# Head-norm factors and their selectors held on 128 partitions instead of 48

## The chip, the cores and the metric

The kernel runs on one core of one Trainium2 chip. It is written in a tile framework that orders the instructions of each engine and places the semaphores. The metric is the device time of one execution in microseconds (us); the time of a kernel is the median of several runs. PE is TensorE (its weight loads are listed apart, as PEld), DVE is VectorE, ACT is ScalarE, SP issues most of the transfers.

## The reference

The program is a first block (attention with dilated windows, a state-space branch and a feed-forward part, all over 256 positions of width 1024) and then a second block of two layers over two streams, x and a context c, of 256 positions each. What matters here is in the mixers of the second block: each head of the queries and keys is normalized over its own 64 (or 64 and 32) features before it is rotated and used.

```
def rms_norm(x, gain=None):
    xf = x.astype(jnp.float32)
    y = xf * lax.rsqrt(jnp.mean(xf * xf, axis=-1, keepdims=True) + EPS)
    if gain is not None:
        y = y * gain.astype(jnp.float32)
    return y.astype(x.dtype)
...
    aq = apply_rope2d(rms_norm(aq.reshape(B, S, A_HEADS, HEAD_DIM), a_q_norm), *rope)
    ak = apply_rope2d(rms_norm(ak.reshape(B, S, A_KV_HEADS, HEAD_DIM), a_k_norm), *rope)
...
    bq = diff_qk(bq, b_q_norm, rope)
    bk = diff_qk(bk, b_k_norm, rope)
...
    dq = rms_norm(dq.reshape(B, S, D_HEADS, HEAD_DIM), d_q_norm)
    dk = rms_norm(dk.reshape(B, S, D_HEADS, HEAD_DIM), d_k_norm)
```

## The kernel before

Activations lie with the features on the partitions and the 256 positions in the free dimension, one tile of 128 features x 256 positions per block. A projection is a row of units. Each unit takes one 128 x 1024 slab of weights (loaded by SP, split into a high part on ACT, line 120, and a low part on DVE, line 121) and multiplies it on TensorE in three products per block of the contraction (lines 139, 140 and 141): 512 columns wide where both streams are taken together, 256 where one is, and 320 or 256 columns in the value projections (lines 1153 to 1155, and 1510 to 1512 for `c_v`).

The mixers `mix_ab` (layer 0) and `mix_cd` (layer 1) run the head norms, class `HeadNorm`, as steps that are queued behind the units (`K.later`) and so fall between the products of later units on TensorE:

- `square_sums`: small products over the squares of a block (line 1035, 2 columns) give the sum of squares of each of its two heads, for each position.
- `spread`: the reciprocal roots of all heads of a group, with positions on the partitions, are transposed (line 1044) to one row per head, `n` rows (10, 8 or 2). `K.split` writes a high part to rows 0 to `n` and a low part to rows 32 to 32+`n` of a tile of the ring `rh`. All other rows hold zeros, written once by `stacked`.
- `finish`: one product per output with a selector of ones and zeros spreads each head's factor over its partitions, in a PSUM tile `pt` (two buffers, which the transposes use too), and DVE multiplies the block by it, at once with its gain (line 1061), or after the rotation (lines 1065 to 1069).

```
            cs = slice(i * 128 + rr.start, i * 128 + rr.stop)
            nc.tensor.matmul(r, self.sel[:, cs], self.r, start=True, stop=True)
            if rope is None:
                nc.vector.scalar_tensor_tensor(o, o, gain[:m], r, op0=ALU.mult, op1=ALU.mult)
```

This product, line 1059, contracts over the partitions of the two tiles, 48. Its moving operand is `rh`, 256 columns, and its stationary operand the selector, `m` columns wide. There are 64 such products. In `mix_ab` there are 26, all with m = 128. In `mix_cd` there are 38: 8 for `dk` and 4 for `dq` with m = 128, 2 for `kr` and 8 for the queries `cq` with m = 96, and 16 for `kn` with m = 64, two per block since a block's two heads go to different places of `kc`.

The selectors are loaded by `head_selectors` from the ACT queue (line 1083) and cast on DVE (line 1084), once in `mix_ab` and twice in `mix_cd`; the ring of four tiles is cleared on ACT (line 1095) in each mixer. The order of the work on each engine comes from the framework and doesn't depend on these sizes.

Of the kernel before, what the change touches and what calls it, by code (L numbers as in the profile page):

```python
# [9 lines left out]
F32R = mybir.dt.float32r  # L10
# [6 lines left out]
T = 256  # L17
# [1058 lines left out]
def head_selectors(K, pool, width, rows, n):  # L1076

    nc, A = K.nc, K.A
    at, n2 = COLS[f"sum{width}"]
    sums = K.cols[:rows, at:at + n2]  # L1080
    raw = K.raw_p.tile([128, 1024], F32, name="wraw")
    sel = pool.tile([48, n * 128], F32R, name=f"sel{width}")
    nc.scalar.dma_start(raw[:48, :n * 128], A[f"sel{width}"])
    nc.vector.tensor_copy(sel, raw[:48, :n * 128])
    return sums, sel


def stacked(K, pool):

    zero = K.t1("zero")  # L1090
    K.nc.vector.memset(zero, 0.0)
    ring = []
    for i in range(4):
        ring.append(pool.tile([48, T], F32R, name=f"rh{i}"))
        K.nc.scalar.copy(ring[i], zero[:48])
    return ring


# [70 lines left out]
def mix_ab(K, streams):  # L1169
# [14 lines left out]
    rctx = ExitStack()  # L1184
    rp = K.pool(rctx, "abr", 1)
    s64, sel64 = head_selectors(K, rp, 64, 128, 5)
    ring = stacked(K, rp)
    cos, sin = K.t1("cos"), K.t1("sin")
    nc.scalar.dma_start(cos, A["rope_cos"])
# [209 lines left out]
def mix_cd(K, streams):  # L1399
# [28 lines left out]
    tctx = ExitStack()  # L1428
    tp = K.pool(tctx, "cdt", 1)
    s64, sel64 = head_selectors(K, tp, 64, 128, 5)  # L1430
    s96, sel96 = head_selectors(K, tp, 96, 96, 4)
    ring = stacked(K, tp)

    rank = {("q", "x"): 6, ("k", "x"): 2, ("k", "c"): 2}
# [304 lines left out]
def constants():  # L1739
    import numpy as np  # L1740
    f = np.float32
    c = {}
    i = np.arange(128)
    c["ident"] = np.eye(128, dtype=f)
    c["tri"] = (i[:, None] <= i[None, :]).astype(f)
    for g, d in ((1, 4), (2, 16)):
        seg = T // d
        ok = (i[:, None] // seg == i[None, :] // seg) & (i[:, None] >= i[None, :])
        c[f"mask{g}"] = np.where(ok, 0.0, NEG).astype(f)

    def bucket(dist):
        dist = np.asarray(dist)
        big = 16 + (np.log(np.maximum(dist, 1).astype(f) / f(16)) / f(math.log(2048 / 16)) * f(16)).astype(np.int32)
        return np.where(dist < 16, dist, np.minimum(big, 31))

    oh = np.zeros((33, 896), f)
    for g, (c0, n, off, d) in enumerate(((0, 383, 255, 1), (384, 255, 127, 4), (640, 255, 127, 16))):
        u = np.arange(n)
        oh[np.where((off - u >= 0) & (off - u <= 128), bucket(np.clip(off - u, 0, 128) * d), 32), c0 + u] = 1.0
    c["onehot"] = oh  # L1760
    sel = np.zeros((8, 512), f)
    for h in range(8):
        sel[h, h * 64:h * 64 + 64] = 1.0
    c["sel"] = sel
    for name, rows, n in (("sel64", [64, 64], 5), ("sel96", [64, 32], 4)):
        sel = np.zeros((48, n, 128), f)
        for b in range(n):
            at = 0
            for e, r in enumerate(rows[:2]):
                sel[[2 * b + e, 32 + 2 * b + e], b, at:at + r] = 1.0  # L1770
                at += r
        c[name] = sel.reshape(48, n * 128)
    t = np.arange(T)

    def rope(dim):
        nf = dim // 4
        inv = (f(10000.0) ** (-np.arange(nf, dtype=f) / f(nf))).astype(f)
        ang = np.concatenate([(t // 64).astype(f)[:, None] * inv, (t % 64).astype(f)[:, None] * inv], axis=-1)
        cos, sin = np.cos(ang.astype(np.float64)).astype(f), np.sin(ang.astype(np.float64)).astype(f)
        full = lambda a, sign: np.stack([sign * a.reshape(T, 2, nf), a.reshape(T, 2, nf)], axis=2).reshape(T, dim).T  # L1780
        return full(cos, 1), full(sin, -1)

    cos, sin = rope(64)
    c["rope_cos"], c["rope_sin"] = np.tile(cos, (2, 1)), np.tile(sin, (2, 1))
    cos, sin = rope(32)
    c["mla_cos"] = np.concatenate([np.ones((64, T), f), cos])
    c["mla_sin"] = np.concatenate([np.zeros((64, T), f), sin])
    q, k = i[:, None], i[None, :]
    c["amask"] = np.stack([np.where(k + 128 - q <= 128, 0.0, NEG), np.where(q + 128 - k <= 128, 0.0, NEG)], 1).astype(f)
    cq = np.tile(np.arange(64), 2)[:, None]  # L1790
    ck = np.tile(np.arange(64), 4)[None, :]
    start = np.clip(cq - 8, 0, 48)
    c["dmask"] = np.where((ck >= start) & (ck < start + 16), 0.0, NEG).astype(f)
    return {k: np.ascontiguousarray(v, dtype=f) for k, v in c.items()}


def prepare(inp):
    import numpy as np
    f = np.float32
    I = {k: np.asarray(v) for k, v in inp.items()}  # L1800
    out = constants()
    feat = lambda a: np.ascontiguousarray(a.reshape(T, KB, 128).transpose(2, 1, 0))
    out["x"], out["ctx"] = feat(I["x"][0]), feat(I["ctx_2"][0])
# [101 lines left out]
```

## Time and profile before

| | |
|---|---|
| median of 3 runs | 2502.96 us (2500.68 to 2505.42) |
| profiled execution | 2511.2 us, of which the span of the program's instructions is 2509.1 us |
| TensorE | busy 2440.5 us, 97% of the span |
| VectorE, ScalarE, GpSimd | busy 1641.9, 1067.5 and 20.6 us |
| mean granted TensorE clock | 0.986 of full speed |

The profiled execution is a single one, 8.2 us above the median; 2.1 us of its time lie outside its span. Busy time of TensorE is modelled: a matmul's record ends when its result is expected, and the next one's begins before that, so the spacing of starts tells more than the durations.

### The profile page before, as it was taken

How to read it: one execution, taken by the hardware profiler on the slowest of the kernel's cores; microseconds unless marked ns; L12 is line 12 of the kernel's file. 1: busy time of each engine (PE TensorE's matmuls, PEld its weight loads, DVE VectorE, ACT ScalarE, POOL GpSimd, SP SyncE). 2: the span in 40 equal slices, each digit the busy share in tenths (PEclk: the TensorE clock that was granted, in tenths of full speed). 3: DMA queues.
4: the chain of work that ended last, by engine and by line, in shares of the span. 5: the costliest groups of instructions: out<-in, count | busy, mean ns of one | idle time of the engine just before them, and what ended most of it. 6: DMA issues, size and time to landing. Idle time of an engine off the chain costs nothing.

```text
span 2509.1 us, 38385 instructions
## 1 busy us (share of the span) xinstructions
PE 2440.5 (97%) x15104; PEld 2097.5 (84%) x15104; DVE 1641.9 (65%) x3012; ACT 1067.5 (43%) x1934; POOL 20.6 (1%) x30
## 2 busy tenths in 40 slices
PE   6999999999999999999999999999999999999999
PEld 5999899999888888886598888887888888866999
DVE  4667787787855675768757666657545455767555
ACT  4667565545522222536743222243222234555443
POOL 1000000000000000000000000000000000000000
PEclk9999899999999999999899999999999999999999
DMA  8555455676444554331025555434555422332554
GB/s 248 161 154 168 137 168 186 203 250 223 160 155 143 162 177 127 122 125 51 1 68 158 161 160 160 155 97 148 171 166 161 142 87 81 108 91 80 177 185 127
DMA packets 117252, 363.83 MB, mean 145 GB/s; under 512 B 21170, under 2 KB 28658, under 8 KB 117072
## 3 DMA queue, kind: packets, MB, share of 16 engines
q1 hardware_dynamic: 114512, 355.73, 44.8%
q0 software_dynamic: 1280, 3.45, 0.7%
q8 instruction: 119, 1.95, 0.3%
q10 hardware_dynamic: 1280, 2.20, 0.3%
q14 instruction: 61, 0.50, 0.1%
HBM read 359.33 MB, written 3.82 MB: 145 GB/s over the span
## 4 chain that ended last, share of the span: by engine, by line
PE 69%; DVE 4%; ACT 2%; issue 1%; DMA 0%; ACTq 0%; DVEq 0%; SPq 0%
PE pm L139 20%; PE pm L140 20%; PE pm L141 20%; PE pt L1128 1%; PE pa L1035 1%; DVE wl L121 1%; PE pm L1327 1%; PE pt L1059 1%; PE pa L1579 1%; PE pm L1587 1%; DVE al L362 1%; PE pa L1343 1%; DVE y L357 1%; PE pm L1267 1%; PE pa L1304 0%
## 5 line engine op out<-in xcount | busy, mean ns | idle before, releaser
L139 PE MATMUL pm<-ah,wh 128*128 128x256 f32 (+2 forms) x3096 | 1007.7, 328 | 25.3 <-ACT ah L361 11.0
L140 PE MATMUL pm<-al,wh 128*128 128x256 f32 (+2 forms) x3096 | 1001.8, 324 | 1.5 <-DVE al L362 1.5
L141 PE MATMUL pm<-ah,wl 128*128 128x256 f32 (+2 forms) x3096 | 999.9, 324 | 0.0
L120 ACT CAST wh<-wraw 128x1024 fp32r<-128x1024 f32 (+4 forms) x535 | 540.4, 1013 | 1028.8 <-PE pm L140 833.4
L121 DVE TENSOR_TENSOR wl<-wraw,wh 128x1024 fp32r<-128x1024 f32 (+4 forms) x535 | 627.4, 1176 | 245.9 <-ACT wh L120 243.4
L139 PEld LDWEIGHTS pm<-ah,wh 128*128 128x128 f32 (+1 forms) x3096 | 587.2, 191 | 87.4 <-ACT ah L361 12.5
L140 PEld LDWEIGHTS pm<-al,wh 128*128 128x128 f32 (+1 forms) x3096 | 591.2, 191 | 56.1 <-DVE al L362 2.8
L141 PEld LDWEIGHTS pm<-ah,wl 128*128 128x128 f32 (+1 forms) x3096 | 588.8, 190 | 52.9 <-issue 1.7
L140 PE MATMUL pm<-hl,wh 128*128 128x512 f32 (+1 forms) x934 | 316.5, 339 | 0.4 <-DVE hl L126 0.4
L139 PE MATMUL pm<-hh,wh 128*128 128x512 f32 (+1 forms) x934 | 316.0, 338 | 0.7 <-DVE xx L449 0.7
L141 PE MATMUL pm<-hh,wl 128*128 128x512 f32 (+1 forms) x934 | 315.9, 338 | 0.0
L989 DVE SCALAR_TENSOR_TENSOR junk<-wraw,cactc 128x1024 f32<-128x1024 f32 x112 | 137.1, 1224 | 187.7 <-DMA wraw<-w_mod 187.5
L989 DVE SCALAR_TENSOR_TENSOR junk<-wraw,cactx 128x1024 f32<-128x1024 f32 x144 | 176.0, 1222 | 40.9 <-DMA wraw<-w_mod 38.3
L140 PEld LDWEIGHTS pm<-hl,wh 128*128 128x128 f32 x934 | 176.4, 189 | 22.2 <-DVE hl L126 0.6
L139 PEld LDWEIGHTS pm<-hh,wh 128*128 128x128 f32 x934 | 175.7, 188 | 22.4 <-issue 0.8
L141 PEld LDWEIGHTS pm<-hh,wl 128*128 128x128 f32 x934 | 175.6, 188 | 21.5
L125 ACT CAST hh<-g 128x512 fp32r<-128x512 f32 (+1 forms) x113 | 59.3, 526 | 183.8 <-DVE g L419 183.8
L419 DVE TENSOR_TENSOR g<-g,pm 128x512 f32<-128x512 f32 (+1 forms) x113 | 64.0, 566 | 69.8 <-PE pm L141 67.9
L126 DVE TENSOR_TENSOR hl<-g,hh 128x512 fp32r<-128x512 f32 (+1 forms) x113 | 63.8, 566 | 0.3
L449 DVE SCALAR_TENSOR_TENSOR xc<-pm,mcol0c,xc 128x256 f32<-128x256 f32 x56 | 26.9, 481 | 56.0 <-PE pm L141 55.9
L415 ACT ACTIVATE g<-pm 128x512 f32<-128x512 f32 (+1 forms) x116 | 56.0, 487 | 1.4 <-PE pm L141 1.4
L1128 PEld LDWEIGHTS pt<-ident,e 128*128 128x128 f32 x272 | 30.7, 145 | 22.1 <-issue 18.8
(423 smaller groups left out, 2243.4 us busy)
## 6 DMA issues: line engine op xcount, KB each, us to landing
wraw<-w_mod SPq DMA_DIRECT2D x144, 512.0 KB, 3.9
wraw<-f1g SPq DMA_DIRECT2D x44, 512.0 KB, 3.7
wraw<-f1u SPq DMA_DIRECT2D x44, 512.0 KB, 4.2
wraw<-f2g SPq DMA_DIRECT2D x44, 512.0 KB, 3.7
wraw<-f2u SPq DMA_DIRECT2D x44, 512.0 KB, 4.0
wraw<-f1d SPq DMA_DIRECT2D x32, 512.0 KB, 4.2
wraw<-f2d SPq DMA_DIRECT2D x32, 512.0 KB, 3.6
wraw<-w_xbc SPq DMA_DIRECT2D x24, 512.0 KB, 3.6
```

Source lines behind the costliest of these rows:

```text
L120: nc.scalar.copy(h[:, :f], raw[:, :f])
L121: nc.vector.tensor_tensor(lo[:, :f], raw[:, :f], h[:, :f].bitcast(F32), op=ALU.subtract)
L125: self.nc.scalar.copy(h, src)
L126: self.nc.vector.tensor_tensor(lo, src, h.bitcast(F32), op=ALU.subtract)
L139: nc.tensor.matmul(out, h[:, c], ah, start=first, stop=False)
L140: nc.tensor.matmul(out, h[:, c], al, start=False, stop=False)
L141: nc.tensor.matmul(out, lo[:, c], ah, start=False, stop=last)
L415: nc.scalar.activation(half(g["g"], s), p, AF.Silu)
L419: nc.vector.tensor_tensor(t, t, p, op=ALU.mult)
L449: self.nc.vector.scalar_tensor_tensor(x, p, gate, x, op0=ALU.mult, op1=ALU.add)
L989: nc.vector.scalar_tensor_tensor(junk, raw, 1.0, K.cact[s], op0=ALU.mult, op1=ALU.mult, accum_out=K.mcol[layer, s][:, j:j + 1])
L1128: nc.tensor.transpose(p[:, j * 128:(j + 1) * 128], b, K.ident)
```

## The change

The tiles of the ring `rh` and of the selectors get 128 partitions instead of 48. The arrays `sel64` and `sel96` in memory get 128 rows, the added ones zero, so the loads, the casts and the clearing are over 128 partitions too. The product of line 1059 then contracts over 128 partitions, of which 80 hold zeros on both sides. Its result is the same sum. No instruction is added, removed or moved on any engine: the lists of before and after differ only in the shapes of the casts, the clearing and the three loads, and in the operands of the 64 products.

```
-    sel = pool.tile([48, n * 128], F32R, name=f"sel{width}")
-    nc.scalar.dma_start(raw[:48, :n * 128], A[f"sel{width}"])
-    nc.vector.tensor_copy(sel, raw[:48, :n * 128])
+    sel = pool.tile([128, n * 128], F32R, name=f"sel{width}")
+    nc.scalar.dma_start(raw[:, :n * 128], A[f"sel{width}"])
+    nc.vector.tensor_copy(sel, raw[:, :n * 128])
...
-        ring.append(pool.tile([48, T], F32R, name=f"rh{i}"))
-        K.nc.scalar.copy(ring[i], zero[:48])
+        ring.append(pool.tile([128, T], F32R, name=f"rh{i}"))
+        K.nc.scalar.copy(ring[i], zero)
...
-        sel = np.zeros((48, n, 128), f)
+        sel = np.zeros((128, n, 128), f)
...
-        c[name] = sel.reshape(48, n * 128)
+        c[name] = sel.reshape(128, n * 128)
```

## Rows read from the trace of the kernel before

**Rows 1.** The page: busy time and share of each engine.
```profile
PE 2440.5 (97%) x15104; PEld 2097.5 (84%) x15104; DVE 1641.9 (65%) x3012; ACT 1067.5 (43%) x1934; POOL 20.6 (1%) x30
```

**Rows 2.** Windows: us, busy (count) PE, PEld, DVE, ACT, POOL, PE clock, DMA share, GB/s.
```profile
1088.00:1153.00 65.00, 64.87 (x356) 53.96 (x355) 44.42 (x137) 17.48 (x42) 0.00 (x0) 1.00 0.21 74
1153.00:1300.00 147.00, 140.23 (x807) 94.65 (x806) 101.60 (x286) 97.14 (x242) 0.00 (x0) 0.95 0.09 29
2130.00:2220.00 90.00, 90.00 (x623) 76.91 (x622) 60.95 (x161) 41.88 (x101) 0.00 (x0) 1.00 0.35 112
```

**Rows 3.** Line 1059: durations in ns (min/median/max), starts, forms.
```profile
L1059 PE MATMUL pt<-rh,sel x64: 275/357/386, 1090.7 to 2216.9; 48*128 48x256 f32 x38, 48*64 48x256 f32 x16, 48*96 48x256 f32 x10
```

**Rows 4.** Timeline of TensorE in mix_cd, a selector product among 256-column products: start, duration.
```profile
2151.60 0.28 PE L140 MATMUL pm<-lq,wh 128*96 128x256 f32 x1
2151.81 0.38 PE L1059 MATMUL pt<-rh,sel 48*128 48x256 f32 x1
2152.12 0.36 PE L141 MATMUL pm<-hq,wl 128*96 128x256 f32 x1
2152.32 0.28 PE L139 MATMUL pm<-hq,wh 128*96 128x256 f32 x1
```

**Rows 5.** Timeline of TensorE in mix_ab, a selector product among 320-column products.
```profile
1145.17 0.31 PE L1154 MATMUL pa<-wh,al 128*128 128x320 f32 x1
1145.41 0.38 PE L1059 MATMUL pt<-rh,sel 48*128 48x256 f32 x1
...
1145.97 0.30 PE L1153 MATMUL pa<-wh,ah 128*128 128x320 f32 x1
```

**Rows 6.** Timeline of TensorE in mix_ab, a pair of selector products before a 512-column unit.
```profile
1097.67 0.50 PE L1059 MATMUL pt<-rh,sel 48*128 48x256 f32 x2
...
1098.44 0.40 PE L140 MATMUL pm<-al,wh 128*128 128x512 f32 x1
```

**Rows 7.** Timeline of TensorE, a product over 96 rows behind one over 128.
```profile
2153.96 0.28 PE L141 MATMUL pm<-hq,wl 128*96 128x256 f32 x1
2154.08 0.50 PE L1035 MATMUL pa<-cols,sq 96*128 96x2 f32 x4
```

**Rows 8.** Timeline of TensorE, a 64-wide selector product (kn).
```profile
2162.59 0.28 PE L139 MATMUL pm<-hq,wh 128*96 128x256 f32 x1
2162.80 0.33 PE L1059 MATMUL pt<-rh,sel 48*64 48x256 f32 x1
2163.06 0.36 PE L140 MATMUL pm<-lq,wh 128*96 128x256 f32 x1
2163.26 0.28 PE L141 MATMUL pm<-hq,wl 128*96 128x256 f32 x1
```

**Rows 9.** Timeline of TensorE: products 64 and 32 wide over all 128 rows, in block 1.
```profile
90.40 0.28 PE L141 MATMUL pm<-ah,wl 128*128 128x256 f32 x1
90.61 0.88 PE L607 MATMUL pm<-pts,vt 128*64 128x128 f32 x12
...
112.19 0.28 PE L141 MATMUL pm<-ah,wl 128*32 128x256 f32 x1
112.31 0.38 PE L542 MATMUL pt<-ident,v 128*128 128x128 f32 x2
```

**Rows 10.** Timeline of TensorE, the one selector pair beside products over 64 rows.
```profile
1137.46 0.38 PE L1059 MATMUL pt<-rh,sel 48*128 48x256 f32 x1
1137.47 0.48 PE L1267 MATMUL pm<-ka,qac 64*128 64x256 f32 x1
```

**Rows 11.** Timelines of DVE and TensorE: the end of one use of `pt`, a later selector product.
```profile
1146.78 0.48 DVE L1061 SCALAR_TENSOR_TENSOR kb<-kb,bkg,pt 128x256 f32<-128x256 f32 x1 [0.53 <-PE pt L1059]
...
1147.95 0.38 PE L1059 MATMUL pt<-rh,sel 48*128 48x256 f32 x1
```

**Rows 12.** Waits of the weight loads in mix_ab (us in total, times, longest).
```profile
PEld pt L1044 <- DVE rs L329: 0.5, 2, 0.4
```

**Rows 13.** Line 1083, the three loads of selectors: issue in ns, starts.
```profile
L1083 ACTq DMA_DIRECT2D wraw<-sel x3: 331/337/337, 988.2 to 2028.5; - x3
```

## The prediction

> **What bounds the kernel.** I read the page first, then the two stretches in which the selector products run, then TensorE's timeline there, start by start. The page has TensorE busy for 97% of the span, far above the others [rows 1]. A busy share alone proves little, since the records' ends are modelled, so I looked at the stretches: 1088 to 1153 us (`mix_ab`) and 2130 to 2220 us (`mix_cd`). TensorE is busy for 64.87 of 65 us and for all of 90, at the full granted clock, while VectorE has 44.42 and 60.95 us of work, ScalarE 17.48 and 41.88, and the transfer engines 0.21 and 0.35 of theirs [rows 2]. So time saved on TensorE there shortens the program, unless something that it waits for doesn't move up with it.
>
> Inside those stretches the reader should look at starts. Ordinary 256-column products follow each other every 0.117 us (14 of them from 2152.32 to 2153.96) [rows 4, 7]. A selector product breaks the row. It starts 0.21 us after the product before it, the next one 0.31 later, and the one after that 0.20 later: 0.72 us for three places that are worth 0.35 [rows 4]. Its own duration in the list of lines, 0.275 to 0.386 us [rows 3], does not show this, because most of the loss is in the neighbours.
>
> I read the three intervals so: the product ahead is let out before the selector product may begin (0.09 over the pitch), then the selector is loaded with nothing running beside it and its 256 columns are let out (0.19 over), and the next weights are again loaded in the open (0.08 over). A product over 96 rows does not do this: it starts 0.12 us behind its neighbour over 128 [rows 7]. So what sets the break is the 48 rows, and 96 are already treated as 128.
>
> **The change, part by part.** I price each break by the spacing it removes, with the selector product itself staying at 0.117.
>
> - 16 lone products beside 96-wide products or 96 wide themselves (8 `dk`, 8 `cq`): 0.72 - 0.35 = 0.37 us each [rows 4], 5.9 us.
> - 16 lone products, 128 wide beside 128-wide weights (14 in `mix_ab`, the last two of `dq`): 0.80 us from 1145.17 to 1145.97 [rows 5], against 2 x 0.147 + 0.117 = 0.41 (the 320-column pitch is an estimate, 0.117 x 320/256). 0.39 us each, 6.2 us.
> - 7 pairs that stand together (5 in `mix_ab`, `kr`, the first two of `dq`): from the first selector to the second product behind the pair 0.77 us [rows 6], against 2 x 0.117 + 0.234 = 0.47 (512 columns, estimated likewise). 0.30, and up to 0.09 for the entry as in rows 4; I take 0.37. 2.6 us.
> - The pair at 1137.46 stands among products over 64 rows, which now share its arrangement: one of them starts 0.01 us after the selector, beside it [rows 10]. With 128 rows TensorE has to change over there and back, at 0.1 to 0.2 us a time by rows 4, so up to 0.6 us lost. Soon after, the transposes of line 1044 wait for VectorE, 0.5 us in total in this stretch [rows 12], and that chain doesn't start from these products; I let the wait cover the loss. 0, and -0.6 without that cover.
> - The 16 `kn` products become 128 rows x 64 columns. A break costs 0.21 + 0.26 + 0.20 - 0.35 = 0.32 us there now [rows 8]. Products of 128 x 64 stand in block 1, and the first of them starts 0.21 us behind its 128 x 128 neighbour; a 32-wide row is left without any break, after 0.12 [rows 9]. So 64 columns break the row as 48 rows do. I take 0; the upper bound is 16 x 0.32 = 5.1 us.
> - Three loads with 128 rows instead of 48, 3 casts and 8 clearings. The loads stand at 988 to 2028 us [rows 13], the added data is 80 rows x 1792 columns x 4 bytes = 0.57 MB, in all 5 us of transfers at the 112 GB/s of the second stretch [rows 2], where their engines are busy for about a third of the time; the selectors are first used at 1090.7 [rows 3], some 100 us after their load. The engines' work goes by the columns, which stay. 0, covered by that lead.
>
> The sum is 5.9 + 6.2 + 2.6 = 14.7 us. From this go waits that appear because TensorE comes earlier. The nearest is `pt` with two buffers: a selector product needs the buffer of the last but one, which VectorE gives back at 1146.78 + 0.48 = 1147.26, and it starts at 1147.95 [rows 11]. That is 0.69 us of slack, and two breaks removed are 0.78. VectorE itself starts sooner as the selector's result comes sooner, so the loss is between 0 and 0.1 us at the 10 products of the tail of `mix_ab` and the 8 of `dk`: 0 to 1.8. I take 0.7, nearer to the lower end, since the result is no longer preceded by an open load.
>
> That leaves 14.0 us. The profiled execution takes 2511.2 us and would take 2497.2, with a span of 2495.1. It is 8.2 us above the median of the runs, so for the median I predict 2502.96 - 14.0 = **2489.0 us**. Bounds of the terms alone: 14.7 - 1.8 - 0.6 = 12.3 us saved at least, 14.7 + 5.1 = 19.8 at most.
>
> **A rule against it.** Rows first: the same three starts cost 0.72 us with a 48-row product in them and 0.35 without [rows 4], and 96 rows cost nothing [rows 7]. The Trainium skill, TensorE: Matmul & The Clock Gate, LDWEIGHTS (loading the stationary operand), says that the time of a weight load goes by its columns and that 32 rows take as long as 128; with only this the change would save nothing and the time would stay at 2503. No row here shows the load's time alone, since the durations in rows 3 are modelled; the starts show a break that this rule doesn't know. The skill's TensorEngine Tiling, Key Properties, has one: changing the tiling mode, not merely the tile, drains the engine, and 48 rows would need its mode of 64 rows. By that page 32 columns are a mode of their own as well, which the exit in rows 9 does not bear out; so for `kn` I go by the 64-column row, not by the page.
>
> **The rivals.**
> - *kn is freed too.* If the break goes by the rows alone when a product stands singly, the 16 `kn` products gain 5.1 us more: 2484. For it: the 32-wide row without a break [rows 9]. Against: the 64-wide one with it. Chance 0.10.
> - *VectorE takes over.* In `mix_ab` it has 44 of 65 us of work [rows 2], but the rotations come in bunches, and two transposes of line 1044 already wait for it [rows 12]. If it can't follow in the tail, the ten lone products there give back their 3.9 us, and the single rotations of `cq` some 1.5: about 8.6 us saved, 2494. Chance 0.10.
> - *Nothing changes.* The break belongs to what line 1059 does (a new wait, another PSUM buffer), not to its rows: 2503. Against: line 1035 in rows 7 has waits of its own and no break. Chance 0.04.
> - *Slower, by the clock.* Outside the stretches the granted clock falls after waits: 0.95 over 147 us of attention [rows 2], that is about 15 us at 1.2 GHz, costing half of it. TensorE reaches the attention 6 to 7 us sooner relative to whatever grants its clock; if such falls get longer, each us of them costs 0.5. It decides from 28 us more at 1.2 GHz, and to end slower by 5 us it takes 38; the whole span has some 70 now (1 - 0.986, twice, of 2509). Chance 0.02: 2508.
>
> **The numbers.** The forecast, 12 to 16 us saved, has 0.74; its own range is 2486.5 to 2491.5. The range that should hold 8 times in 10 reaches to `kn` freed below and to VectorE's case above, with some us for the clock: 2483 to 2496. A measurement can tell 0.2%, 5.0 us, from no change. All of the forecast and the first two rivals lie beyond that, less a little for runs in which the clock eats part of it: faster 0.91, same 0.07, slower 0.02.
>
> **What would show it.** Right: the starts around a selector product at 0.12 us with its load during the product before it; the stretches 1088 to 1153 and 2130 to 2220 shorter by 6 to 7 us each; the 64-wide products still at 0.21, 0.26, 0.20; the pair at 1137 costlier than now. Wrong: breaks of the same size around 128 rows, or selector products spaced by VectorE's use of `pt`, with waits of PE on lines 1061 and 1069.

## The result and the profile after

| | before | after |
|---|---|---|
| median of 8 runs each, us | 2506.34 (2500.68 to 2513.03) | 2490.62 (2479.57 to 2498.00) |
| ratio, 95% interval | 1 | 0.9934 [0.9912, 0.9956] |
| profiled execution, us | 2511.2 | 2491.84 |
| its span, us | 2509.1 | 2489.7 |

The change makes the kernel faster by 0.66%, 15.7 us on the medians (11 to 22 by the interval). The forecast was 2489.0 us in a range of 2483 to 2496, so the time came out 1.6 us above it, and 14.0 us had been forecast as saved. That the two agree so well is partly luck: two terms were wrong by more than their difference, in opposite directions, and the median of the kernel before is 3.4 us higher over these 8 runs than over the 3 from which the forecast counted down (2502.96).

The page's first part, after (answers to [rows 1]): TensorE has 19.1 us less of busy time, and VectorE, ScalarE and GpSimd have what they had within 1 us.

```profile
PE 2421.4 (97%) x15104; PEld 2089.8 (84%) x15104; DVE 1641.9 (66%) x3012; ACT 1068.4 (43%) x1934; POOL 20.6 (1%) x30
```

Line 1059 in the two stretches, of before and then of after: count, durations in ns, first and last start, forms.

```profile
L1059 PE MATMUL pt<-rh,sel x26: 277/381/386, 1090.7 to 1151.9; 48*128 48x256 f32 x26
L1059 PE MATMUL pt<-rh,sel x38: 275/352/384, 2133.1 to 2216.9; 48*64 48x256 f32 x16, 48*128 48x256 f32 x12, 48*96 48x256 f32 x10
```
```profile
L1059 PE MATMUL pt<-rh,sel x26: 276/298/387, 1093.8 to 1149.1; 128*128 128x256 f32 x26
L1059 PE MATMUL pt<-rh,sel x38: 277/282/387, 2130.5 to 2203.7; 128*64 128x256 f32 x16, 128*128 128x256 f32 x12, 128*96 128x256 f32 x10
```

From the first selector product to the last, `mix_ab` went from 61.3 to 55.3 us and `mix_cd` from 83.8 to 73.3: 6.0 and 10.6 us (16.55 in all from the unrounded starts, 61.27 to 55.29 and 83.83 to 73.26). The rest of the span's 19.4 us is not the change's: the stretch ahead of the first selector is 3.2 us longer in this execution, the one between the two is equal within 0.2 us, and the one behind the last is 6.2 us shorter (292.1 to 286.0). What the last is made of stands at the end.

TensorE's timeline around two selector products, 128 and 64 wide (answers to [rows 4] and [rows 8]): every start is 0.11 to 0.12 us behind the one before, and nothing around them is spread.

```profile
2153.96 0.28 PE L140 MATMUL pm<-lq,wh 128*96 128x256 f32 x1
2154.08 0.28 PE L1059 MATMUL pt<-rh,sel 128*128 128x256 f32 x1
2154.19 0.28 PE L141 MATMUL pm<-hq,wl 128*96 128x256 f32 x1
2154.31 0.28 PE L139 MATMUL pm<-hq,wh 128*96 128x256 f32 x1
...
2156.30 0.28 PE L139 MATMUL pm<-hq,wh 128*96 128x256 f32 x1
2156.41 0.28 PE L1059 MATMUL pt<-rh,sel 128*64 128x256 f32 x1
2156.53 0.28 PE L140 MATMUL pm<-lq,wh 128*96 128x256 f32 x1
```

The weight loads (PEld) show what the break was. Here are the selector's load and the one behind it, first before (the place of [rows 4]), then after (the place just shown):

```profile
2151.81 0.18 PEld L1059 LDWEIGHTS pt<-rh,sel 48*128 48x128 f32 x1 [0.16 <-issue]
2152.12 0.16 PEld L141 LDWEIGHTS pm<-hq,wl 128*96 128x96 f32 x1
```
```profile
2153.96 0.19 PEld L1059 LDWEIGHTS pt<-rh,sel 128*128 128x128 f32 x1
2154.08 0.16 PEld L141 LDWEIGHTS pm<-hq,wl 128*96 128x96 f32 x1
```

Before, both loads start at the same time as the products that they serve (2151.81 and 2152.12), so nothing covers them. After, each starts with the product ahead of its own (2153.96 and 2154.08, for products at 2154.08 and 2154.19). That is the sign that the prediction named, a load during the product before. Of the 64 selector loads, 56 start within 0.002 us of their own product before, and 8 after; the other 8 of before stand behind another selector product of 48 rows.

So the breaks are gone at the places whose gain was forecast, and at the `kn` products too, whose gain was forecast as nothing. A part of them is left at some places, which the experiments come to.

### The profile page after: what moved, and what is told of

Read it like the earlier page. It is cut to its first block, busy times and chain, and to the rows that moved or that the text cites. A ratio compares the mean times of both kernels' runs of the same rounds, so it can differ in the third digit from the quotient of the medians.

```text
span 2489.7 us, 38385 instructions
## 1 busy us (share of the span) xinstructions
PE 2421.4 (97%) x15104; PEld 2089.8 (84%) x15104; DVE 1641.9 (66%) x3012; ACT 1068.4 (43%) x1934; POOL 20.6 (1%) x30
## 4 chain that ended last, share of the span: by engine, by line
PE 69%; DVE 3%; ACT 2%; issue 1%; DMA 0%; ACTq 0%; DVEq 0%; SPq 0%
PE pm L139 20%; PE pm L140 20%; PE pm L141 20%; PE pt L1128 1%; PE pa L1035 1%; PE pm L1327 1%; PE pa L1579 1%; DVE wl L121 1%; PE pm L1587 1%; DVE al L362 1%; PE pa L1343 1%; DVE y L357 1%; PE pm L1267 1%; PE pa L1304 0%; PE pt L1059 0%
## 5 line engine op out<-in xcount | busy, mean ns | idle before, releaser
L139 PEld LDWEIGHTS pm<-ah,wh 128*128 128x128 f32 (+1 forms) x3096 | 588.0, 191 | 86.4 <-ACT ah L361 12.5
L313 DVE TENSOR_TENSOR acc<-acc,sq 128x256 f32<-128x256 f32 x105 | 42.3, 419 | 11.0 <-ACT sq L312 10.8
```

What stands on the lines that cost most here:

```text
L139: nc.tensor.matmul(out, h[:, c], ah, start=first, stop=False)
L313: nc.vector.tensor_tensor(self.acc[key], self.acc[key], sq, op=ALU.add)
```

## The experiments

Two words first. The pitch is the distance from start to start in an unbroken row of products. And fp32r is the type of the selectors, of `rh` and of the projections; a product in it leaves one record in the trace, a product in plain fp32 two (32 for the 16 `kn` products, in the experiment that makes them plain).

Theory: a product over 48 rows (fp32r) puts TensorE into another arrangement than its neighbours over 128, and each change-over drains the row. Rivals: the gain comes from the tiles (their loads, casts and clearings) and not from the rows that the product reads; it goes up gradually with the rows; and, for `kn`, that 64 columns break the row whatever the rows.

**The tiles without the rows.** All tiles have 128 partitions, and the products read 48 of them.

```
-nc.tensor.matmul(r, self.sel[:, cs], self.r, ...)
+nc.tensor.matmul(r, self.sel[:48, cs], self.r[:48], ...)
```

> Tiles, loads, casts and clearing on 128 partitions as in the changed kernel; all 64 products read only the first 48 partitions. Theory (all of the change lies in the rows of the products): first to last selector product 61.3 us in mix_ab and 83.8 in mix_cd, as before, and the time that of before within 0.3%. Rival (the larger loads or casts cost or save time): the time differs from before by more than 0.3%, or a stretch by more than 0.5 us.

Measured: 2503.14 us, ratio to before 0.9999 [0.9976, 1.0021]. First to last selector took 61.3 and 83.8 us, as before. So the larger loads, casts and clearings cost nothing that can be measured (one cast took 0.475 us before and 0.484 after, one clearing 0.399 and 0.400), and the whole of the gain lies in the rows that the product reads.

**96 rows, and 64.** The same edit with `:96` and with `:64`.

> As in the changed kernel, but all 64 products read the first 96 partitions. Theory (the break belongs to an arrangement for up to 64 rows, 96 already count as 128): 55.3 us in mix_ab and 73.3 in mix_cd, within 0.5 us each, and a time about 0.6% below before. Rival (only a full 128 rows avoid the break): 61.3 and 83.8 us and the time of before.

> As in the changed kernel, but all 64 products read the first 64 partitions. Theory (an arrangement for up to 64 rows, the same for 48 and 64): 61.3 us in mix_ab and 83.8 in mix_cd, within 0.5 us each. Rival (the cost falls gradually as more rows are used): between before and after, some 60 and 81 us.

Measured: 96 rows give 2489.04 us, ratio 0.9927 [0.9903, 0.9951], and stretches of 55.3 and 73.0 us, those of 128 rows. 64 rows, in a single execution, give 2503.37 us and 61.3 and 85.3 us, those of 48. Here is `mix_cd` with 64 rows: the form has 64, the median duration is that of before, 352 ns (282 with 128 rows).

```profile
L1059 PE MATMUL pt<-rh,sel x38: 275/352/579, 2131.5 to 2216.8; 64*64 64x256 f32 x16, 64*128 64x256 f32 x12, 64*96 64x256 f32 x10
```

The 1.5 us over the 83.8 that were expected for 64 rows stand at 2147 to 2150 us, where the granted clock is at 0.50 in this execution; they are not the rows'. So the cost has two levels, the same for 48 and 64 rows and none for 96 and 128; it is not gradual. What the rows change is when the load starts, and not how long it takes: with 128, 96 and 64 columns its median record is 183, 156 and 129 ns over 48 rows (before), and 188, 164 and 134 over 128 (after). Where it is open, its columns show in the starts: with 48 rows it takes 0.31, 0.28 and 0.26 us from a lone selector product of 128, 96 and 64 columns to the next product. The Trainium skill, TensorE: Matmul & The Clock Gate, LDWEIGHTS (loading the stationary operand), says that the time of a load goes by its columns and not by its rows. The trace agrees for the load itself, and by that rule alone all of these kernels would take the same time; 61.3 us against 55.3 is what it leaves out. The Trainium skill, TensorEngine Tiling (Array Packing), Key Properties, says that a change of tiling mode drains TensorE, which agrees with the two levels; which mode a product uses, no record here shows.

**`kn` alone on 48 rows.** 16 products of the changed kernel go back.

```
+k = 48 if m == 64 else 128
-nc.tensor.matmul(r, self.sel[:, cs], self.r, ...)
+nc.tensor.matmul(r, self.sel[:k, cs], self.r[:k], ...)
```

> All as in the changed kernel, but the 16 kn products (64 wide) read only the first 48 partitions of the ring and the selector again. Measured from the first to the last selector product of each mixer, which took 61.3 us (mix_ab) and 83.8 us (mix_cd) before and 55.3 and 73.3 us after. Theory (a break comes with 48 rows, and 128 rows x 64 columns standing singly have none): mix_ab stays at 55.3 us, mix_cd rises to 76.5 to 78.3 us, with starts of 0.21, 0.26 and 0.20 us around each kn product. Rival (kn gained nothing by itself, the rest of mix_cd gained more than I counted): mix_cd stays within 0.5 us of 73.3.

Measured in a single execution: 2509.59 us; `mix_ab` 55.3 us as in the changed kernel, `mix_cd` 77.7, which is 4.46 us longer (unrounded). The rows are those of [rows 8] again, 0.21 ahead, 0.25 and 0.20 behind (the line has moved by one):

```profile
2165.28 0.28 PE L139 MATMUL pm<-hq,wh 128*96 128x256 f32 x1
2165.49 0.33 PE L1060 MATMUL pt<-rh,sel 48*64 48x256 f32 x1
2165.74 0.36 PE L140 MATMUL pm<-lq,wh 128*96 128x256 f32 x1
2165.94 0.28 PE L141 MATMUL pm<-hq,wl 128*96 128x256 f32 x1
```

So the 16 `kn` products gained 4.46 us, 0.28 each, of the 5.1 that were given as the upper bound. The total of this single execution, 2509.59, is above that of before although 12 us of the gain are kept; its granted clock is 0.982 over the span, and 0.50 from 248 to 272 us. A single total cannot tell 5 us here, and the stretches can.

**Why the 64-wide row of block 1 misled.** The products of [rows 9] come in pairs, for output partitions 0 to 63 and 64 to 127, and their tiles are plain fp32; `kn` is single and fp32r. The profile prints f32 for both types. Two kernels separate the two. In the first, 25 selector products of 128 columns are made as block 1's are:

```
+for a in (0, 64):
+    h = slice(cs.start + a, cs.start + a + 64)
+    nc.tensor.matmul(p[a:a + 64, :T], self.sel[:, h].bitcast(F32), self.r.bitcast(F32), ...)
```

> The 25 selector products that are 128 wide and carry no rotation (13 in mix_ab, 12 in mix_cd) are each made as two plain-fp32 products of 128 rows by 64 columns of weights, for output partitions 0 to 63 and 64 to 127, as block 1 lays out its 64-wide products. Asked is what breaks the row in block 1, where a 128x64 product starts 0.21 us behind its 128x128 neighbour, while the 64-wide kn products of the changed kernel start after 0.12. Theory A, the second place at column 64 (two products side by side) is an arrangement of its own: the first half starts 0.20 to 0.22 us behind the 128x128 product before it, the halves start within 0.02 us of each other, and the next 128-wide product again has an open load (0.20 or more behind). Theory B, the arrangement goes by rows alone: the first half starts 0.12 us behind, the halves one after the other. By either the first-to-last stretches get longer, by 0.3 to 0.5 us for each product: mix_ab 59 to 62 us (55.3 in the changed kernel), mix_cd 77 to 79.5 (73.3). So the starts decide, not the total, which should be 2498 to 2504 us.

In the second, the `kn` products stay single at partition 0 and become plain fp32:

```
+if m == 64:
+    a, b = a.bitcast(F32), b.bitcast(F32)
```

> As the changed kernel, but the 16 kn products (128 rows by 64 columns of weights, alone, at partition 0) are plain fp32 instead of fp32r; nothing stands at column 64. Theory A (the break of block 1 comes from the second place at column 64): the kn products start 0.12 us behind their neighbours as now, take a second pass of 0.1 to 0.2 us, and the product behind follows without an open load; first to last selector in mix_cd is 73.3 + 16 x 0.1 to 0.2 = 74.9 to 76.5 us. Theory B (64 wide in plain fp32 is what breaks the row): entry 0.20 to 0.22, exit 0.2 or more, mix_cd 76.5 to 79. mix_ab stays at 55.3 by both.

Measured, in a single execution each: the pairs give 60.4 and 77.5 us, and a total of 2493.43, below the 2498 to 2504 expected (the order of the stream changes with this edit, and a few other products leave the two stretches, so that the starts decide). The single fp32 products give 81.0 us in `mix_cd`, with the same other products in it, 7.7 more than the changed kernel and above both expectations, and 2497.91 us in total. TensorE's timeline, first of the pairs, then of the single ones:

```profile
1123.55 0.31 PE L1161 MATMUL pm<-wl,ah 128*128 128x320 f32 x1
1123.70 0.30 PE L1159 MATMUL pm<-wh,ah 128*128 128x320 f32 x1
1123.93 0.65 PE L1062 MATMUL pt<-rh,sel 128*64 128x256 f32 x4
1124.51 0.42 PE L1160 MATMUL pm<-wh,al 128*128 128x320 f32 x1
```
```profile
2164.35 0.28 PE L141 MATMUL pm<-hq,wl 128*96 128x256 f32 x1
2164.47 0.28 PE L139 MATMUL pm<-hq,wh 128*96 128x256 f32 x1
2164.68 0.65 PE L1062 MATMUL pt<-rh,sel 128*64 128x256 f32 x2
2165.25 0.36 PE L140 MATMUL pm<-lq,wh 128*96 128x256 f32 x1
```

Both break the row at entry: 0.23 where 0.147 is the pitch of 320 columns, and 0.21 where 0.118 is that of 256. The two halves of a pair start within 0.01 us of each other, side by side as theory A had it. But the single product breaks the row without anything at column 64, so the second place is not needed: plain fp32 with 64 columns is enough, and the same 64 columns in fp32r are not. The single product costs 0.48 us (7.7 / 16), where theory B had 0.36 at most. It has two records (x2), and 0.57 us pass from its start to the next product, against 0.12 in fp32r: 0.27 from its first pass to its second and 0.31 from there. So about half of the 0.48 is the second pass and the rest is the break. What the engine sets differently for the two types, no run shows.

**What the selector places still cost.** Counting the intervals ahead of, at and behind each selector product against the pitch, 1.2 us are left in `mix_ab` and 1.3 in `mix_cd` (7.2 and 12.5 before). A part is the wait for a `pt` buffer, as here in the tail of `mix_ab` after the change: the selector product starts 0.03 us later than the 320-column pitch of 0.147 allows, and the one behind it 0.10 later than 256 columns take.

```profile
1145.12 0.30 PE L1154 MATMUL pa<-wh,al 128*128 128x320 f32 x1
1145.30 0.38 PE L1059 MATMUL pt<-rh,sel 128*128 128x256 f32 x1
1145.52 0.31 PE L1155 MATMUL pa<-wl,ah 128*128 128x320 f32 x1
```

Giving the products the four-buffer pool instead:

```
-p = K.pt.tile([128, 512], F32, name="pt")
+p = K.psum()
```

> As the changed kernel, but the selector products write tiles of the four-buffer pool pm instead of the two-buffer pool pt. Asked is what the 2.5 us are that the selector places still cost over an unbroken row (1.2 in mix_ab, 1.3 in mix_cd). Theory A, the wait for a pt buffer: the places at which the selector product starts 0.05 us after VectorE gives the buffer back lose that wait, and first to last selector gets shorter by 0.6 to 1.2 us in each stretch: mix_ab 54.1 to 54.7, mix_cd 72.0 to 72.7. Rival, VectorE itself is late (its rotations come in bunches): the wait only moves to the products that need the pm buffers, mix_ab 55.2 to 55.6 and mix_cd 73.2 to 74.5. In total at most 2.5 us faster than the changed kernel, which one look at the total can't tell.

Measured in a single execution: 2489.97 us. First to last selector is 51.3 and 75.2 us, but the scheduler orders the stream anew with this edit, so that these do not compare. By the places themselves the excess in `mix_ab` falls from 1.2 to 0.6 or 0.7 us, by how one counts at the new neighbours: there the wait was the buffer's. In `mix_cd` it rises to some 3.5. A wait of TensorE there, and a window (busy time and count of each engine, clock, DMA):

```profile
PE pm L1059 <- DVE rh L126: 0.7, 1, 0.7
```
```profile
2137.50:2145.00 7.50, 6.79 (x45) 6.55 (x45) 4.85 (x13) 4.79 (x13) 0.00 (x0) 0.77 0.29 96
```

A selector product now stands so early that it waits 0.7 us for its factors, and the clock falls to 1.2 GHz right behind that wait, from 2139.6 to 2143.1 us. Neither theory as written: the buffer was about half of what is left in `mix_ab`, and the single total shows no gain in the whole.

**The same edit elsewhere.** In block 1, 12 products of line 658 read 8 rows in plain fp32. They got 128 rows with zeros too; the scheduler changes the order around them.

```
+nc.gpsimd.memset(comb["sel"], 0.0)
+nc.gpsimd.memset(ssd["ub"][:, 0:3], 0.0)
-nc.tensor.matmul(p[:, :T], comb["sel"][:, ...], comb["rm"][:, g], ...)
+nc.tensor.matmul(p[:, :T], comb["sel"][:, ...], comb["all"][:, g], ...)
```

> As the changed kernel, and the 12 combine products of block 1 (line 658, 8 rows, plain fp32, 245.9 to 261.1 us) get 128 rows as well, by zeros. Now a pair of them starts 0.21 us behind its neighbour, its four passes follow after 0.32, 0.22 and 0.22, the next product after 0.30 and the one after that after 0.22: 1.48 us for six places. Theory A (8 rows are a third case of the same break): entry 0.12, passes 0.22 apart, exit 0.12 to 0.22, about 1.1 us; some 0.3 to 0.4 us for each pair that isn't waiting for VectorE, 1 to 2 us in all. Rival B (plain fp32 breaks the row whatever its rows): entry 0.20 and the same 1.4 to 1.5 us. Rival C: from 254 us on VectorE bounds these products (spacings of 0.35 to 0.59), so that the stretch from the first to the last of them stays at 14.7 to 15.2 us.

A single execution gave 2477.08 us. The first and last combine products were 8.1 us apart, against 15.2 in the changed kernel, so rival C was wrong as well as B. This was repeated with timing, beside the changed kernel itself and a version of the same order with 64 rows (`[:64]` on both operands).

> The kernel of e8_combine128 again, timed. In its one look the stretch around the combine products was some 6 us shorter and the granted clock stayed at 1.00 from 245 to 270 us, where every other kernel so far (8-row combine products) shows 0.50 for 5 to 15 us after them. Theory A, that this repeats: ratio to the kernel before 0.990 to 0.9925 (0.9934 for the changed kernel), the clock 0.97 to 1.00 in 250 to 270 us. Theory B, that the look was one with luck in the clock and in the pitch: ratio 0.993 to 0.995 and a fall of the clock behind the combine products as before.

> The changed kernel itself, unedited, beside e9_combine128_timed on the same chip. Ratio 0.992 to 0.995 as on record; the granted clock falls to 0.50 between 252 and 265 us again. If it does not fall here, the fall does not belong to the 8-row products.

> As e8_combine128, with the same order of instructions on every engine, but the combine products read 64 rows of their padded tiles. It asks whether the rows or the changed order kept the clock up and took the breaks out. Theory A, the rows: pairs start 0.20 us behind their neighbour again, with passes at 0.32, 0.22, 0.22 and exits of 0.30 and 0.22, and the granted clock may fall behind them as with 8 rows; first to last combine product 10 to 15 us (8.1 in e8_combine128). Theory B, the order alone: entry 0.12, 8 to 8.5 us, clock 1.00.

Measured on one chip: 2479.02 us with 128 rows in the combine products, ratio 0.9887 [0.9869, 0.9905], below what either theory gave; 2484.80 us for the changed kernel, 0.9914 [0.9888, 0.9940], with the clock at 0.50 from 254 to 268 us again; 2495.21 us in a single execution with 64 rows. The windows of the changed kernel, of the version with 128 rows and of that with 64 (the figure ahead of the last two is the granted clock):

```profile
245.00:270.00 25.00, 24.39 (x129) 19.54 (x128) 17.89 (x41) 8.96 (x19) 0.00 (x0) 0.80 0.19 60
```
```profile
245.00:270.00 25.00, 23.41 (x181) 21.51 (x180) 24.30 (x51) 13.31 (x27) 0.00 (x0) 1.00 0.37 106
```
```profile
245.00:270.00 25.00, 23.01 (x67) 16.22 (x68) 13.46 (x30) 6.88 (x17) 0.00 (x0) 0.54 0.13 43
```

In the same 25 us TensorE gets through 129, 181 and 67 products. The break itself is plain in the starts; first 8 rows in the changed kernel, then 128:

```profile
247.84 0.28 PE L140 MATMUL pm<-al,wh 128*128 128x256 f32 x1
248.04 1.12 PE L658 MATMUL pt<-ub,gts 8*128 8x256 f32 x4
249.10 0.39 PE L141 MATMUL pm<-ah,wl 128*128 128x256 f32 x1
249.32 0.28 PE L139 MATMUL pm<-ah,wh 128*128 128x256 f32 x1
```
```profile
248.87 0.28 PE L139 MATMUL pm<-ah,wh 128*128 128x256 f32 x1
248.98 1.02 PE L661 MATMUL pt<-ub,gts 128*128 128x256 f32 x4
249.66 0.47 PE L140 MATMUL pm<-al,wh 128*128 128x256 f32 x1
249.96 0.28 PE L141 MATMUL pm<-ah,wl 128*128 128x256 f32 x1
```

From the product ahead to the second one behind, 1.48 us become 1.09. The entry is at the pitch now (0.11); 0.30 us are still left between the two products behind, and no run asked why. But of the 7.1 us between the two kernels (15.2 and 8.1 from the first combine product to the last) about 3.3 are the granted clock, by an estimate: in the changed kernel it is at 0.50 from 254.5 to 264.8 us, and half of the 6.6 us up to the last combine product at 261.1 is lost. Whether rows or luck set the clock in the version with 64 rows, the last run asked:

> The kernel of e11_combine64 again, timed: the order of e9_combine128_timed on every engine, with 64 rows instead of 128 in the 12 combine products. In its one look the granted clock fell already during the wait ahead of the first combine product and stayed at 0.50 until 270 us; first to last combine product took 18.4 us (8.1 with 128 rows). Theory A, the rows lead to it: the clock is at 0.50 for 8 us or more between 245 and 275 us again, and the ratio to the kernel before is 0.992 to 0.996 (0.9887 with 128 rows). Theory B, that look had bad luck with the clock: no fall there, first to last combine product 10 to 11.5 us (8.1 and 12 breaks at 0.2 to 0.3), ratio 0.988 to 0.991.

Measured, on another chip: 2488.38 us, ratio 0.9925 [0.9898, 0.9953], and no fall of the clock in the profiled execution: 1.00 from 245 to 275 us. The combine products of this run and of the one before it, both over 64 rows:

```profile
L661 PE MATMUL pt<-ub,gts x24: 376/376/480, 246.2 to 256.4; 64*128 64x256 f32 x24
```
```profile
L661 PE MATMUL pt<-ub,gts x24: 581/631/792, 247.0 to 265.4; 64*128 64x256 f32 x24
```

At the full clock they take 10.2 us, 8.1 with 128 rows: 2.1 us are the rows', as theory B had it. The 18.4 us of the execution before were the clock's, in the same program. So theory A falls by its first sign: 64 rows alone don't bring the fall. The ratio would fit A (0.992 to 0.996), but its interval reaches over B's (0.988 to 0.991) as well, so it decides nothing. The fall came here in all 10 profiled executions with 8 rows (before, after and eight experiments), in one of two with 64 rows, and in neither of two with 128, which have a shorter fall, of some 3.4 us, later, at 288 and 320 us. The order around the products differs between the first group and the other two, and whether it or the rows keep the clock up stays open. Against the kernel before, the version with 128 rows is faster by 1.1%. The interval of that lies below the one on record for the changed kernel, [0.9912, 0.9956], and overlaps the one taken beside it from 0.9888 to 0.9905; that it is the faster of the two is likely, not settled.

## Why the prediction held

**What bounds the kernel, and the break: right.** TensorE's starts were the right thing to read, and 48 rows the cause; the versions that read 48, 64 and 96 rows show it. So was the reading of the three intervals: the selector's load and the next one were open, which the rows of the weight loads show directly. The prediction held that no row shows a load's time alone; the trace has these records. That 96 rows count as 128, read off [rows 7], is confirmed by time.

**Loads, casts and clearings, 0: right.** 0.9999 [0.9976, 1.0021] with them alone.

**The pair at 1137.46, 0 to -0.6: right, at the small end.** The timeline after (answers to [rows 10]) has the 64-row products behind the pair instead of beside it.

```profile
1136.98 0.95 PE L1035 MATMUL pa<-cols,sq 128*128 128x2 f32 x8
1137.78 0.48 PE L1059 MATMUL pt<-rh,sel 128*128 128x256 f32 x2
1138.19 1.13 PE L1267 MATMUL pm<-ka,qac 64*128 64x256 f32 x8
1139.26 0.42 PE L1153 MATMUL pa<-wh,ah 128*128 128x320 f32 x1
```

From the last product of line 1035 to line 1153 it takes 1.59 us, 1.51 before: 0.08 lost.

**`kn`, 0: wrong, and the first rival was right.** The step that failed is "So 64 columns break the row as 48 rows do". The row it was read from is a plain fp32 product, and `kn` is fp32r. The term measures 4.46 us, which is why `mix_cd` got shorter by 10.6 us and not by the 6 to 7 that were named as a sign. The rival had 0.10, and its mechanism is the one that the runs bear out, for fp32r; its time, 2484, did not come, since the next term fell short; [rows 9] held the evidence for it, a 32-wide fp32r row without a break, and the kernel's code the difference in type.

**The waits, -0.7 (0 to -1.8): mis-sized, -2.6.** The lone products and the pairs were to bring 14.7 us. They brought 16.55 - 4.46 = 12.1, so 2.6 are missing. Of the excess that is left at the selector places (1.2 and 1.3, ahead of the experiment on `pt`), about 2.0 lie at these products and 0.4 at `kn`; the other 0.6 of the 2.6 are not traced. Two parts of the 2.0 were named by the runs: the buffers (0.5 or 0.6 us in `mix_ab`), and the pairs, which were costed as if nothing were left. A pair stands behind the two-column products of line 1035, and its second product starts 0.20 us behind its first (answers to [rows 6]; the two starts of the x2 row are 1100.58 and 1100.78):

```profile
1100.58 0.48 PE L1059 MATMUL pt<-rh,sel 128*128 128x256 f32 x2
1100.90 0.39 PE L139 MATMUL pm<-ah,wh 128*128 128x512 f32 x1
1101.13 0.39 PE L140 MATMUL pm<-al,wh 128*128 128x512 f32 x1
```

First to second product behind the pair: 0.55 us, where 0.47 was the estimate and [rows 6] have 0.77. The selector products of 96 columns behind line 1035 do the same, with 0.17 to 0.18, and one of 64 columns with 0.15. I read it as a load in the open behind products too short to cover one; that it goes by the columns of the selector speaks for it, but no run changed line 1035, so it is argued, not shown.

**The sum.** 12.1 + 4.46 = 16.55 us on the path, against 14.0: the two errors are +4.46 and -1.9.

**The other rivals.** VectorE did not take over: the stretches shrank by what TensorE gave back. That line 1059 itself breaks the row is out, since the same line with 96 rows does not. The slower clock did not come as a rule: the attention behind `mix_ab` has a granted clock of 0.94 over 147 us, against 0.95 in [rows 2], and the whole span 0.984 against 0.986, but 0.987 in the second profiled execution of the changed kernel.

```profile
1149.20:1296.20 147.00, 140.75 (x804) 95.02 (x804) 102.44 (x289) 97.10 (x242) 0.00 (x0) 0.94 0.10 29
```

## What to carry to other kernels

Read TensorE by the distance from start to start of the products around an odd-shaped one, not by its own duration: here a 48-row product cost 0.37 us, and its own recorded duration showed 0.10 of that (0.38 us in [rows 4] against 0.28 after). Look also at when the weight load starts: with the product ahead it is covered, with its own product it is not. Zeros up to the neighbours' row count are free when the tile is loaded early, and 96 rows did as well as 128; 64 did as badly as 48. Before a price is taken from another place of the same kernel, see that it has the same type as well as the same shape: fp32r and plain fp32 print alike in the profile, and the number of records for each product (x2 for a plain one) tells them apart.

## What the hardware showed beside this

The pitch of a 256-column stream has two values for the same program. In the last FFN, with no wait and the clock at 1.00, windows of 23 us hold 205 products in the first execution of the version with 128 rows in the combine products, and 197 in the second, with the same kernel:

```profile
2310.00:2333.00 23.00, 23.00 (x205) 23.00 (x204) 14.07 (x18) 10.79 (x17) 0.00 (x0) 1.00 0.71 233
```
```profile
2310.00:2333.00 23.00, 23.00 (x197) 23.00 (x196) 13.61 (x18) 10.98 (x18) 0.00 (x0) 1.00 0.72 228
```

The profiled executions of before and after happen to differ in just this way:

```profile
2327.00:2350.00 23.00, 23.00 (x197) 23.00 (x197) 15.70 (x20) 14.19 (x22) 0.00 (x0) 1.00 0.62 206
```
```profile
2314.30:2337.30 23.00, 23.00 (x205) 23.00 (x204) 15.67 (x20) 15.07 (x22) 0.00 (x0) 1.00 0.65 210
```

That is 0.1168 and 0.1122 us each, 7.2 us over the 1583 steps of that stretch, and more than the 6.2 by which the end of the span is shorter after the change. Of the 14 profiled executions, 4 have the long pitch there (before, `kn` on 48 rows, and the timed versions with 128 and 64 rows in the combine products). What sets it, no run shows. Together with falls of the granted clock, which come at other lengths in each execution, it is large enough for a good part of the scatter (2479.57 to 2498.00 us for the changed kernel alone), and it is why a stretch between two landmarks tells more here than a total.
